# A hybrid attention and gMLP block: own buffer rings for the raw tiles and operands of a Strassen MLP, and an output projection with one PSUM bank for each half

## The chip, the cores and the metric

The kernel runs on one core of a Trainium2 chip. The metric is device time in microseconds (us) of one execution, as the median of several runs. One execution was also taken by the hardware profiler; its rows are what the text reads.

## What is computed

One layer over x of 2048 rows by 1024 columns, float32. Cut to what matters here:

```python
h = rmsnorm(x, norm_mix_g)
q, k, v, u, vg = split(h @ w_in)                      # five parts of 512 columns
a_out = stick_breaking_attention(q, k, v)             # 8 heads of 64, causal
b_out = spatial_gating(gelu(u), gelu(vg), ...)        # 8 groups of 64
mix = concat(rmsnorm(a_out, g[:512]), rmsnorm(b_out, g[512:]))
x = x + mix @ w_out                                   # 1024 x 1024
h = rmsnorm(x, norm_mlp_g)
x = x + square(relu(h @ w_up)) @ w_down               # 1024 -> 4096 -> 1024
return rmsnorm(x, norm_final_g)
```

## The kernel before

The rows are worked in four chunks of 512 (`TC`), each of four blocks of 128 (`NTB`). Matmul operands are split into a high and a low float32r part: `split` (lines 78 to 85) copies the high part on ScalarE (ACT, line 81) and subtracts for the low part on VectorE (line 82). `mm3` (lines 87 to 91) then makes three matmuls of 512 columns: high by high, high by low, low by high.

Work is written as Python generators, and `together(main, side, ratio)` steps a side generator `ratio` times for each `yield` of the main one. The program framework sorts each engine's instructions when the program is built, beginning from program order; an instruction whose inputs and buffer are ready may go ahead of an earlier one that still waits. All loads discussed here are issued on the queue of SyncE (SP), in the order that came out of this.

The order is: input projections of chunks 0 and 1; projections of chunks 2 and 3 with attention as the side; then, still beside attention, `Out(0)` and `Out(1)` (output projection and second norm), `up_plain` (first MLP layer of chunks 0 and 1), `Out(2)`, and `down_plain`; then `Out(3)` beside the rest of `down_plain`; and last the MLP of chunks 2 and 3 by a scheme of seven products (Strassen), `up_seven` and `down_seven`, with nothing beside it.

`Out` has three parts. `operands` loads `a_d` (transposed, 512 by 512) and `b_d`, squares `b` with a running sum (line 475), splits `a`, squares `a` (line 479), adds the squares of four tiles on GpSimd (POOL, lines 481 and 482), sums over partitions with a matmul against a column of ones (line 486), makes both inverse roots, multiplies `b`'s by the root of `a`'s mean (lines 490 to 493), scales `b` on ACT (line 498), transposes it on TensorE (line 501) and splits it. `product` loads the residual x (line 527), then for each half of 512 output columns loads both parts of `w_out` (line 512, or line 515 with a split for chunk 0, which also stores the split parts), and for each row block runs 24 matmuls of both parts into one PSUM bank, which VectorE adds to the residual with the scale of `a` (line 543). `turn` normalizes and transposes. A chunk may start only when attention has made the steps of that chunk (the `while steps[0]` loops).

A `Room` hands out buffers from rings by name; a ring serves its tiles in program order, and a tile waits until a slot is free:

```python
rm = Room(None, None, dict(w8=9, s12=1, t8=12, acts=2, t2=2), dict(w8=hx, s12=hx))
```

In the Strassen stages `w8` (nine slots of 8 KB per partition) serves raw tiles, by `raw8`, and operands, by `w8`, alike. `Rights` holds the seven right operands of the up stage, the first of them (`hc[0]`) in two `w8` tiles, the others in `t8`. `Lefts` loads one raw tile of `w_up` for each `q` of 16 (line 717) and makes seven operands in four `w8` pairs. The products of a `q` are 12 matmuls each; `keep_acts` sums and stores the result to `s_d` (lines 583 to 587). `down_seven` has four groups `g` of seven products (`ORDER_D`). Each product loads a raw tile from `s_d` (line 857) and splits it and a `w_down` combination into four `w8` tiles: two for the first half of its contraction, two for the second. It then runs 48 matmuls into four banks, and VectorE adds these to accumulators (lines 826 to 831). At the start of a group POOL makes three differences for each half (lines 847 to 849), later one more (line 851). The raw tiles of `w_down` come from `t8` (line 808), in odd groups half of them from `w8`. `y_d` is loaded at line 819. In the last group the last two products run row block by row block, and `finish` writes the output.

Of the kernel before, what the change touches and what calls it, by code (L numbers as in the profile page):

```python
# [8 lines left out]
F32 = mybir.dt.float32  # L9
F32R = mybir.dt.float32r  # L10
BF16 = mybir.dt.bfloat16
AF = mybir.ActivationFunctionType
ALU = mybir.AluOpType
# [3 lines left out]
P = 128  # L17
# [4 lines left out]
SBW = 512  # L22
DFF = 4096
TC = 512
NTB = TC // P
NC = T // TC
KD = D // P
EPS = 1e-6
# [6 lines left out]
def block_kernel(ctx: ExitStack, tc: tile.TileContext, x, x_t, gmix, w_in, ln_g, ln_b, sgw, sgb,  # L35
                 outg, w_out, gmlp, w_up, w_down, gfin, out):
    nc = tc.nc
# [14 lines left out]
    ones = const.tile([P, 1], F32, name="ones")  # L52
    nc.gpsimd.memset(ones, 1.0)
    mhalf = const.tile([P, NTB], F32, name="mhalf")
# [11 lines left out]
    b_d = dram.tile([T, SBW], F32, name="b_d")  # L66
    wi_d = dram.tile([5, KD // 2, P, 2, 2, 512], F32, name="wi_d")
    wo_d = dram.tile([2, 2, 2, P, 4, 512], F32, name="wo_d")

    def rsqrt_mean(pool, ssq, n, count, tag):  # L70

        m = pool.tile([P, NTB], F32, name=f"{tag}_m", bufs=2)
        nc.vector.tensor_scalar(m[:, :n], ssq, 1.0 / count, EPS, ALU.mult, ALU.add)  # L73
        r = pool.tile([P, NTB], F32, name=f"{tag}_r", bufs=2)
        nc.gpsimd.tensor_tensor(r[:, :n], m[:, :n], mhalf[:, :n], ALU.pow)  # L75
        return r
# [10 lines left out]
    def mm3(ps, lh, ll, rh, rl, first, last, more=False):  # L87

        nc.tensor.matmul(ps, lh, rh, start=first, stop=False, skip_group_check=more)  # L89
        nc.tensor.matmul(ps, lh, rl, start=False, stop=False, skip_group_check=more)  # L90
        nc.tensor.matmul(ps, ll, rh, start=False, stop=last, skip_group_check=more)  # L91
# [332 lines left out]
    class Room:  # L424
# [9 lines left out]
        def w8(self, shape):  # L434
            return self.get("w8", shape, F32R)

        def raw8(self, shape):
            return self.get("w8", shape)

        def t8(self, shape, dtype=F32):  # L440
            return self.get("t8", shape, dtype)
# [13 lines left out]
    def split4(hl, src):  # L455
        for j in range(0, 4, 2):
            split(hl[0][:, j:j + 2, :], hl[1][:, j:j + 2, :], src[:, j:j + 2, :])

    class Out:
# [3 lines left out]
            self.c, self.rm = c, room  # L463

        def operands(self):

            rm, c = self.rm, self.c
            at = rm.t8([4, TC])
            nc.sync.dma_start(at, a_d[:, c * TC:(c + 1) * TC].rearrange("(n p) t -> p n t", p=P))
            st = rm.t8([4, SBW])  # L470
            nc.sync.dma_start(st, b_d[c * TC:(c + 1) * TC, :].rearrange("(n p) d -> p n d", p=P))
            ssq = rm.small("rb_ssq", NTB)
            for tb in range(NTB):
                sq = rm.t4([SBW], BF16)
                nc.scalar.activation(sq, st[:, tb, :], AF.Square, accum_out=ssq[:, tb:tb + 1])
            am = self.am = rm.pair([4, TC])
            split4(am, at)
            yield
            nc.scalar.activation(at, at, AF.Square)
            total = rm.pool.tile([P, TC], F32, name="a_sq", bufs=1)  # L480
            nc.gpsimd.tensor_tensor(at[:, 0:2, :], at[:, 0:2, :], at[:, 2:4, :], ALU.add)
            nc.gpsimd.tensor_tensor(total, at[:, 0, :], at[:, 1, :], ALU.add)
            rb = rsqrt_mean(rm.pool, ssq, NTB, SBW, "rb")
            pssq = rm.ps()
            for tb in range(NTB):
                nc.tensor.matmul(pssq[:, tb:tb + 1], total[:, tb * P:(tb + 1) * P], ones, start=True, stop=True)
            m = rm.small("ra_m", NTB)
            nc.vector.tensor_scalar(m, pssq[:, :NTB], 1.0 / SBW, EPS, ALU.mult, ALU.add)
            ra = rm.small("ra", NTB)
            nc.gpsimd.tensor_tensor(ra, m, mhalf[:, :NTB], ALU.pow)  # L490
            root = rm.small("ra_root", NTB)
            nc.gpsimd.tensor_tensor(root, m, ra, ALU.mult)
            nc.gpsimd.tensor_tensor(rb, rb, root, ALU.mult)
            self.ras = [ra[:, tb:tb + 1] for tb in range(NTB)]
            yield
            bm = self.bm = rm.pair([4, TC])
            for tb in range(NTB):
                nc.scalar.activation(st[:, tb, :], st[:, tb, :], AF.Copy, scale=rb[:, tb:tb + 1])
                ps = rm.ps((P, 4, P))
                for e in range(4):  # L500
                    nc.tensor.transpose(ps[:, e, :], st[:, tb, e * P:(e + 1) * P], ident)
                ts_ = slice(tb * P, (tb + 1) * P)
                split(bm[0][:, :, ts_], bm[1][:, :, ts_], ps)
                yield

        def weights(self, half, part):

# [13 lines left out]
        def product(self):  # L521
            rm, c = self.rm, self.c
            self.ys = []
            for t2 in range(2):
                y = rm.t8([2, D])
                r0 = c * TC + t2 * 2 * P
                nc.sync.dma_start(y, x[r0:r0 + 2 * P, :].rearrange("(n p) d -> p n d", p=P))
                self.ys += [y[:, 0, :], y[:, 1, :]]
            ys = self.ys

            for half in range(2):
                ws = [self.weights(half, part) for part in range(2)]
                hs = slice(half * 512, (half + 1) * 512)
                for tb in range(NTB):
                    ts_ = slice(tb * P, (tb + 1) * P)
                    ps = rm.ps()
                    for part, m in ((0, self.am), (1, self.bm)):
                        for e in range(4):
                            mm3(ps, m[0][:, e, ts_], m[1][:, e, ts_], ws[part][0][:, e, :], ws[part][1][:, e, :],
                                part == 0 and e == 0, part == 1 and e == 3)  # L540
                            if e == 1 or part == 0 and e == 3:
                                yield
                    nc.vector.scalar_tensor_tensor(ys[tb][:, hs], ps, self.ras[tb], ys[tb][:, hs], ALU.mult, ALU.add)
                    if half == 1:
                        nc.sync.dma_start(y_d[c][:, tb, :], ys[tb])
                    yield
                if c == 0:
                    for part in range(2):
                        for i in range(2):
                            nc.sync.dma_start(wo_d[half, part, i], ws[part][i].bitcast(F32))  # L550

        def turn(self):

# [122 lines left out]
    class Rights:  # L676


        def __init__(self, rm):

            self.rm, self.hc = rm, [None] * 7
            self.b11, self.t2, self.b12, self.b21, self.b22 = (rm.raw8([4, TC]) for _ in range(5))
            b11 = self.b11
            for t, src in ((b11, h_d[0][0]), (self.b12, h_d[1][0]), (self.b22, h_d[1][1]), (self.b21, h_d[0][1])):
                nc.sync.dma_start(t, src)
            self.keep(0, b11, rm.w8)
            self.minus(b11, self.b12, b11)
            self.minus(self.t2, self.b22, b11)
            self.minus(self.b12, self.b22, self.b12)
# [21 lines left out]
    class Lefts:  # L711


        def __init__(self, rm, q):
            self.rm, self.pair, self.n = rm, None, 0
            st = rm.raw8([2, 2, 512])
            nc.sync.dma_start(st, w_up[2 * q:2 * q + 2].rearrange("f p (h k) c -> p f h (k c)", h=2))
            a11, self.a12, self.a21, self.a22 = st[:, 0, 0], st[:, 0, 1], st[:, 1, 0], st[:, 1, 1]
            self.a11, self.s = a11, rm.get("s12", [512])
            nc.gpsimd.tensor_tensor(self.s, self.a21, self.a22, ALU.add)  # L720
            self.w0, self.w4 = self.operand(a11), self.operand(self.s)

        def operand(self, src):
            if self.n % 2 == 0:
                self.pair = self.rm.w8([2, 2, 512])
            w = self.pair[:, self.n % 2]
            self.n += 1
            split(w[:, 0, :], w[:, 1, :], src)
            return w
# [64 lines left out]
    class Down:  # L794
# [5 lines left out]
        def load(self, g):  # L800

            self.bs = []
            for h in range(2):
                v = []
                f0 = (8 * g + 4 * h) * P
                for n in range(2):
                    st = self.rm.raw8([4, 512]) if g % 2 and h else self.rm.t8([4, 512])
                    nc.sync.dma_start(st, w_down[f0:f0 + 4 * P, n * 512:(n + 1) * 512].rearrange("(f p) d -> p f d", p=P))
                    st = st.rearrange("p (j e) d -> p j e d", e=2)
                    v += [st[:, :, 0], st[:, :, 1]]  # L810
                self.bs.append([v[0], v[2], v[1], v[3]])
# [190 lines left out]
        for part in (o.operands, o.product, o.turn):  # L1002
            together(part(), down, 0.8)
    hx = ctx.enter_context(tc.tile_pool(name="hx", bufs=1, side="right", reuse_waits="tile"))
    rm = Room(None, None, dict(w8=9, s12=1, t8=12, acts=2, t2=2), dict(w8=hx, s12=hx))
    rights = Rights(rm)
    ahead = Lefts(rm, 0)
    together(down)
# [46 lines left out]
```

## Time and profile before

| | us |
|---|---|
| median of 3 runs (lowest, highest) | 2624.02 (2620.88, 2625.3) |
| the profiled execution, device time | 2620.27 |
| the profiled execution, span of its instructions | 2618.6 |
| TensorE busy | 2454.1 |
| VectorE busy | 1684.6 |
| ScalarE busy | 1158.5 |
| mean granted TensorE clock | 0.972 of full speed |

The span runs from the first to the last instruction of the profiled execution. Busy time counts instructions at work on an engine. The granted clock is what the chip allowed TensorE, as a share of full speed; TensorE is either at its full 2.4 GHz or at 1.2 GHz, so 0.77 in a stretch means that it was at the lower level for 46% of it. PE is TensorE, PEld its weight loads, DVE VectorE, ACT ScalarE, POOL GpSimd, SPq the queue on which SyncE issues transfers.

### The profile page before, as it was taken

To read this page: it belongs to the slowest core of one execution; us is meant where nothing else is said; L and a number is where in the kernel's file an instruction comes from. 1 tells how busy PE (TensorE), PEld (TensorE's weight loads), DVE (VectorE), ACT (ScalarE), POOL (GpSimd) and SP (SyncE) were. 2 spreads that over 40 slices of the span, in tenths; PEclk is the share of its full clock that TensorE was granted. 3 is DMA by queue.
4 is the path that set the end of the run, shared out by engine and by line. 5 is a ranking of instruction groups with operands and counts; after the bars stand their busy time and mean duration, and the time that the engine had idled before them with its cause. 6 is when DMAs were issued, how large, how long until landed. Compare 5 with 4: busy or idle time off the path is not lost. (4 is left out here: it accounts for less than half of the span.)

```text
span 2618.6 us, 30138 instructions
## 1 busy us (share of the span) xinstructions
PE 2454.1 (94%) x11328; PEld 1985.7 (76%) x11328; DVE 1684.6 (64%) x2236; ACT 1158.5 (44%) x2020; POOL 315.4 (12%) x259
## 2 busy tenths in 40 slices
PE   8899898997979999999999899999989999799997
PEld 7787677775757888888877688788767888687875
DVE  3643557868675666666666688635566665468877
ACT  4422335536454555555564454313134544233333
POOL 1100000101010000000010000000023323213330
PEclk9999999998989999999999899999999999999998
DMA  9637788677654343333364633346223344753332
GB/s 374 244 125 219 215 255 261 205 221 224 244 190 157 121 121 121 121 124 122 121 236 162 197 121 113 122 156 241 96 81 142 140 161 149 261 206 116 113 113 113
DMA packets 158225, 446.58 MB, mean 171 GB/s; under 512 B 12544, under 2 KB 28928, under 8 KB 138624
## 3 DMA queue, kind: packets, MB, share of 16 engines
q1 hardware_dynamic: 149744, 417.39, 47.8%
q0 software_dynamic: 4032, 25.17, 2.4%
q10 hardware_dynamic: 4304, 2.10, 0.3%
q8 instruction: 90, 1.47, 0.2%
q14 instruction: 55, 0.45, 0.1%
HBM read 314.59 MB, written 130.02 MB: 170 GB/s over the span
## 5 line engine op out<-in xcount | busy, mean ns | idle before, releaser
L89 PE MATMUL mm<-t,t 128*128 128x512 f32 x1280 | 499.5, 394 | 4.5 <-DVE t L664 4.5
L91 PE MATMUL mm<-t,t 128*128 128x512 f32 x1280 | 502.3, 393 | 0.0
L90 PE MATMUL mm<-t,t 128*128 128x512 f32 x1280 | 501.9, 392 | 0.3 <-DVE t L82 0.3
L359 DVE TENSOR_TENSOR_SCAN pr<-kk,pr,zeros 128x513 f32<-128x513 f32 x192 | 248.3, 1293 | 117.3 <-ACT kk L351 116.9
L351 ACT ACTIVATE kk<-z 128x512 f32<-128x512 f32 (+2 forms) x320 | 171.5, 536 | 334.5 <-PE z L346 187.8
L89 PEld LDWEIGHTS mm<-t,t 128*128 128x128 f32 x1280 | 242.3, 190 | 55.6 <-DVE t L664 4.9
L90 PEld LDWEIGHTS mm<-t,t 128*128 128x128 f32 x1280 | 241.9, 189 | 51.4 <-DVE t L82 1.1
L91 PEld LDWEIGHTS mm<-t,t 128*128 128x128 f32 x1280 | 241.5, 189 | 51.6
L81 ACT ACTIVATE w<-w 128x512 fp32r<-128x512 f32 (+1 forms) x150 | 121.1, 825 | 299.6 <-DMA w<-s_d 172.3
L82 DVE TENSOR_TENSOR w<-w,w 128x512 fp32r<-128x512 f32 (+1 forms) x150 | 176.5, 1191 | 88.7 <-ACT w L81 86.8
L370 PE MATMUL tr<-ident,b 128*128 128x128 f32 x1088 | 186.3, 283 | 43.7 <-DVE aT L82 30.0
L90 PE MATMUL mm<-w,w 128*128 128x512 f32 x512 | 204.1, 399 | 17.3 <-DVE w L82 17.3
L82 DVE TENSOR_TENSOR aT<-tr,aT 128x512 fp32r<-128x512 f32 (+1 forms) x320 | 190.9, 599 | 35.7 <-ACT aT L81 35.6
L89 PE MATMUL mm<-w,w 128*128 128x512 f32 x512 | 201.4, 396 | 12.4 <-ACT w L81 11.5
L81 ACT ACTIVATE aT<-tr 128x512 fp32r<-128x512 f32 (+1 forms) x320 | 172.6, 541 | 90.2 <-PE tr L370 89.7
L91 PE MATMUL mm<-w,w 128*128 128x512 f32 x512 | 202.8, 396 | 0.0
L370 PEld LDWEIGHTS tr<-ident,b 128*128 128x128 f32 x1088 | 133.6, 144 | 90.7 <-DVE aT L82 38.8
L81 ACT ACTIVATE t<-t 128x1024 fp32r<-128x1024 f32 x104 | 105.7, 1060 | 179.1 <-DMA t<-in_w_down 112.8
L353 ACT ACTIVATE b<-z 128x512 f32<-128x512 f32 (+2 forms) x320 | 171.3, 535 | 0.5 <-PE tr L370 0.5
L356 DVE TENSOR_TENSOR_SCAN pr<-kk,zeros 128x128 f32<-128x128 f32 (+3 forms) x128 | 105.5, 826 | 90.8 <-ACT kk L351 90.3
L89 PE MATMUL mm<-t,w 128*128 128x512 f32 x384 | 154.0, 401 | 8.9 <-DVE acts L775 4.7
L388 PE MATMUL av<-aT,vt 128*128 128x512 f32 (+1 forms) x320 | 144.5, 452 | 13.7 <-DMA vt<-v_d 3.5
(192 smaller groups left out, 4629.3 us busy)
## 6 DMA issues: line engine op xcount, KB each, us to landing
w_in<-wi_d SPq DMA_DIRECT2D x40, 1024.0 KB, 8.0
kt<-k_d SPq DMA_DIRECT2D x160, 256.0 KB, 4.9
t<-in_w_down SPq DMA_DIRECT2D x28, 1024.0 KB, 6.6
s_d<-acts SPq DMA_DIRECT2D x16, 1792.0 KB, 6.2
w<-s_d SPq DMA_DIRECT2D x28, 1024.0 KB, 4.8
t<-wo_d SPq DMA_DIRECT2D x24, 1024.0 KB, 8.7
wi_d<-w_in POOLq DMA_DIRECT2D x20, 1024.0 KB, 8.0
vt<-v_d SPq DMA_DIRECT2D x80, 256.0 KB, 2.9
```

The lines of the kernel that those rows point to most:

```text
L81: nc.scalar.activation(hi, src, AF.Copy)
L82: nc.vector.tensor_tensor(lo, src, hi.bitcast(F32), ALU.subtract)
L89: nc.tensor.matmul(ps, lh, rh, start=first, stop=False, skip_group_check=more)
L90: nc.tensor.matmul(ps, lh, rl, start=False, stop=False, skip_group_check=more)
L91: nc.tensor.matmul(ps, ll, rh, start=False, stop=last, skip_group_check=more)
L351: nc.scalar.activation(kk[:, :L], z[:, :L], AF.Sigmoid, scale=-QK_SCALE)
L353: nc.scalar.activation(b[:, :L], z[:, :L], AF.Sigmoid, scale=QK_SCALE)
L356: nc.vector.tensor_tensor_scan(pr[:, L - 1::-1], kk[:, L - 1::-1], zeros[:, :L], 1.0, ALU.mult, ALU.add)
L359: nc.vector.tensor_tensor_scan(pr[:, ::-1], kk[:, ::-1], zeros, carry[tb], ALU.mult, ALU.add)
L370: nc.tensor.transpose(tr[:, tb * P:(tb + 1) * P], bs[tb][:, j * P:(j + 1) * P], ident)
L388: nc.tensor.matmul(av[:, t0:], vt[:, j, :], aT[:, 0, t0:], start=first, stop=False)
```

## The change

In the Strassen stages the nine slots are cut into three rings: five `w8` for operands, two `raw8` for raw tiles, two `x8` for `hc[0]` and, in odd groups of the down stage, for half of the `w_down` raw tiles. The first operand pair of the up stage stands in `raw8`.

In `Out`, the weights of the first product group are asked for first, then `b_d`, then `a_d`. `b` is transposed unscaled, its norm made block by block. The sum of squares of `a` is made by 16 matmuls that accumulate on TensorE. The product runs in four groups, each of one half of the columns and one part of the contraction (`b` first); each row block of a group has a bank of its own for 12 matmuls, and VectorE adds it to the residual with the norm of that part.

```diff
-        def raw8(self, shape):
-            return self.get("w8", shape)
+        def raw8(self, shape, dtype=F32):
+            return self.get("raw8", shape, dtype)
+
+        def x8(self, shape, dtype=F32R):
+            return self.get("x8", shape, dtype)
...
         def operands(self):
-
             rm, c = self.rm, self.c
+            self.rbs = []
+            self.ready = [self.weights(0, 1)]
+            st = rm.t8([4, SBW])
+            nc.sync.dma_start(st, b_d[c * TC:(c + 1) * TC, :].rearrange("(n p) d -> p n d", p=P))
             at = rm.t8([4, TC])
             nc.sync.dma_start(at, a_d[:, c * TC:(c + 1) * TC].rearrange("(n p) t -> p n t", p=P))
-            st = rm.t8([4, SBW])
-            nc.sync.dma_start(st, b_d[c * TC:(c + 1) * TC, :].rearrange("(n p) d -> p n d", p=P))
-            ssq = rm.small("rb_ssq", NTB)
+            bm = self.bm = rm.pair([4, TC])
             for tb in range(NTB):
                 sq = rm.t4([SBW], BF16)
-                nc.scalar.activation(sq, st[:, tb, :], AF.Square, accum_out=ssq[:, tb:tb + 1])
-            am = self.am = rm.pair([4, TC])
-            split4(am, at)
-            yield
-            nc.scalar.activation(at, at, AF.Square)
-            total = rm.pool.tile([P, TC], F32, name="a_sq", bufs=1)
-            nc.gpsimd.tensor_tensor(at[:, 0:2, :], at[:, 0:2, :], at[:, 2:4, :], ALU.add)
-            nc.gpsimd.tensor_tensor(total, at[:, 0, :], at[:, 1, :], ALU.add)
-            rb = rsqrt_mean(rm.pool, ssq, NTB, SBW, "rb")
...
-                nc.scalar.activation(st[:, tb, :], st[:, tb, :], AF.Copy, scale=rb[:, tb:tb + 1])
+                ssq = rm.small("rb_ssq")
+                nc.scalar.activation(sq, st[:, tb, :], AF.Square, accum_out=ssq)
+                m = rm.small("rb_m")
+                nc.vector.tensor_scalar(m, ssq, 1.0 / SBW, EPS, ALU.mult, ALU.add)
+                rb = rm.small("rb", bufs=2 * NTB)
+                nc.gpsimd.tensor_tensor(rb, m, mhalf[:, 0:1], ALU.pow)
+                self.rbs.append(rb)
                 ps = rm.ps((P, 4, P))
                 for e in range(4):
                     nc.tensor.transpose(ps[:, e, :], st[:, tb, e * P:(e + 1) * P], ident)
                 ts_ = slice(tb * P, (tb + 1) * P)
                 split(bm[0][:, :, ts_], bm[1][:, :, ts_], ps)
                 yield
+            am = self.am = rm.pair([4, TC])
+            split4(am, at)
+            nc.scalar.activation(at, at, AF.Square)
+            pssq = rm.ps()
+            for tb in range(NTB):
+                for e in range(4):
+                    nc.tensor.matmul(pssq[:, tb:tb + 1], at[:, e, tb * P:(tb + 1) * P], ones, start=e == 0, stop=e == 3)
+            ra = rsqrt_mean(rm.pool, pssq[:, :NTB], NTB, SBW, "ra")
+            self.ras = [ra[:, tb:tb + 1] for tb in range(NTB)]
+            yield
...
-            for half in range(2):
-                ws = [self.weights(half, part) for part in range(2)]
+            def group(half, part, m, rr):
+                ws = self.ready.pop() if self.ready else self.weights(half, part)
                 hs = slice(half * 512, (half + 1) * 512)
                 for tb in range(NTB):
                     ts_ = slice(tb * P, (tb + 1) * P)
                     ps = rm.ps()
-                    for part, m in ((0, self.am), (1, self.bm)):
-                        for e in range(4):
-                            mm3(ps, m[0][:, e, ts_], m[1][:, e, ts_], ws[part][0][:, e, :], ws[part][1][:, e, :],
-                                part == 0 and e == 0, part == 1 and e == 3)
-                            if e == 1 or part == 0 and e == 3:
-                                yield
-                    nc.vector.scalar_tensor_tensor(ys[tb][:, hs], ps, self.ras[tb], ys[tb][:, hs], ALU.mult, ALU.add)
-                    if half == 1:
+                    for e in range(4):
+                        mm3(ps, m[0][:, e, ts_], m[1][:, e, ts_], ws[0][:, e, :], ws[1][:, e, :], e == 0, e == 3)
+                        if e == 1:
+                            yield
+                    nc.vector.scalar_tensor_tensor(ys[tb][:, hs], ps, rr[tb], ys[tb][:, hs], ALU.mult, ALU.add)
+                    if half == 1 and part == 0:
                         nc.sync.dma_start(y_d[c][:, tb, :], ys[tb])
                     yield
...
+            yield from group(0, 1, self.bm, self.rbs)
+            yield from group(0, 0, self.am, self.ras)
+            yield from group(1, 1, self.bm, self.rbs)
+            yield from group(1, 0, self.am, self.ras)
...
-            self.b11, self.t2, self.b12, self.b21, self.b22 = (rm.raw8([4, TC]) for _ in range(5))
+            self.b11, self.t2, self.b12, self.b21, self.b22 = (rm.get("w8", [4, TC]) for _ in range(5))
...
-            self.keep(0, b11, rm.w8)
+            self.keep(0, b11, rm.x8)
...
-                self.pair = self.rm.w8([2, 2, 512])
+                self.pair = self.rm.raw8([2, 2, 512], F32R) if self.first and self.n == 0 else self.rm.w8([2, 2, 512])
...
-                    st = self.rm.raw8([4, 512]) if g % 2 and h else self.rm.t8([4, 512])
+                    st = self.rm.x8([4, 512], F32) if g % 2 and h else self.rm.t8([4, 512])
...
-    rm = Room(None, None, dict(w8=9, s12=1, t8=12, acts=2, t2=2), dict(w8=hx, s12=hx))
+    rm = Room(None, None, dict(w8=5, raw8=2, x8=2, s12=1, t8=12, acts=2, t2=2),
+              dict(w8=hx, raw8=hx, x8=hx, s12=hx))
```

## Rows read from the trace of the kernel before

**Rows 1.** The page, busy time of TensorE: us, share of the span, instructions.

```profile
PE 2454.1 (94%) x11328; PEld 1985.7 (76%) x11328; DVE 1684.6 (64%) x2236; ACT 1158.5 (44%) x2020; POOL 315.4 (12%) x259
```

**Rows 2.** Busy time by stretch: stretch, length, engines, PEclk, DMA share, GB/s.

```profile
613.00:660.00 47.00, 32.26 (x151) 23.92 (x151) 42.15 (x64) 34.97 (x72) 7.94 (x8) 0.79 0.83 262
725.00:770.00 45.00, 29.95 (x128) 20.76 (x127) 37.29 (x52) 29.09 (x58) 8.08 (x7) 0.77 0.77 252
840.00:1315.00 475.00, 474.94 (x2348) 391.43 (x2348) 307.88 (x390) 265.93 (x504) 8.78 (x8) 1.00 0.39 121
1345.00:1372.00 27.00, 20.58 (x106) 15.63 (x106) 20.45 (x29) 15.52 (x30) 1.94 (x3) 0.94 0.98 352
1975.00:2255.00 280.00, 279.98 (x1221) 228.91 (x1220) 173.68 (x231) 133.53 (x228) 82.11 (x56) 1.00 0.42 149
2255.00:2300.00 45.00, 29.09 (x103) 22.45 (x103) 24.19 (x23) 15.45 (x19) 16.47 (x7) 0.77 0.75 288
2360.00:2385.00 25.00, 22.62 (x98) 17.72 (x97) 22.46 (x17) 7.57 (x9) 18.95 (x6) 1.00 0.24 85
2520.00:2580.00 60.00, 50.16 (x208) 40.57 (x207) 51.30 (x48) 18.71 (x19) 21.55 (x8) 0.91 0.23 84
```

**Rows 3.** Timeline of chunk 1's `Out`: start, us, engine, line, operation, idle before.

```profile
730.64 0.38 SPq L469 DMA_DIRECT2D t<-a_d  x1
...
751.32 1.87 PE L486 MATMUL mm<-ones,a_sq 128*128 128x1 f32 x8 [1.99 <-POOL a_sq L482]
...
756.13 1.95 ACT L498 ACTIVATE t<-t,rb_r 128x512 f32<-128x512 f32 x3 [6.55 <-POOL rb_r L493]
...
771.74 0.86 PE L89 MATMUL mm<-t,t 128*128 128x512 f32 x3
```

**Rows 4.** Timeline of the SP queue in chunk 0's `Out`.

```profile
613.90 0.87 SPq L469 DMA_DIRECT2D t<-a_d  x1
...
640.40 0.46 SPq L515 DMA_DIRECT2D t<-in_w_out  x1
```

**Rows 5.** Timeline of the SP queue from the up stage into the down stage.

```profile
2236.96 0.34 SPq L857 DMA_DIRECT2D w<-s_d  x1
2249.06 0.37 SPq L808 DMA_DIRECT2D t<-in_w_down  x1
...
2272.19 0.37 SPq L587 DMA_DIRECT2D s_d<-acts  x1
2272.64 2.99 SPq L819 DMA_DIRECT2D t<-y_d  x3
2275.68 46.41 SPq L857 DMA_DIRECT2D w<-s_d  x5
```

**Rows 6.** Timeline of ACT, VectorE and TensorE at the start of the down stage.

```profile
2265.58 1.06 ACT L81 ACTIVATE w<-t 128x1024 fp32r<-128x1024 f32 x1 [0.53 <-DMA t<-in_w_down]
...
2272.04 1.21 DVE L82 TENSOR_TENSOR w<-t,w 128x1024 fp32r<-128x1024 f32 x1
...
2273.30 0.79 PE L90 MATMUL mm<-w,w 128*128 128x512 f32 x1 [4.37 <-DVE w L82]
...
2292.49 1.65 PE L89 MATMUL mm<-w,w 128*128 128x512 f32 x3 [11.54 <-ACT w L81]
```

**Rows 7.** Timeline of VectorE in the last group of the down stage.

```profile
2547.63 5.01 DVE L831 TENSOR_TENSOR t<-t,t 128x512 f32<-128x512 f32 x6
```

**Rows 8.** Timeline of VectorE and ACT at a product's end, and beside POOL.

```profile
2304.74 2.73 DVE L828 TENSOR_TENSOR t<-mm,t 128x512 f32<-128x512 f32 x4 [4.04 <-PE mm L91]
2306.11 1.06 ACT L81 ACTIVATE w<-w 128x1024 fp32r<-128x1024 f32 x1 [7.99 <-PE mm L91]
...
2446.18 3.41 DVE L82 TENSOR_TENSOR w<-w,w 128x1024 fp32r<-128x1024 f32 x1
```

**Rows 9.** Timeline of the sums in chunk 2; the evacuations of the product by line.

```profile
1344.59 1.05 PE L486 MATMUL mm<-ones,a_sq 128*128 128x1 f32 x8
...
L543 DVE SCALAR_TENSOR_TENSOR t<-mm,ra,t x32: 741/751/752, 668.8 to 1788.1; 128x512 f32<-128x512 f32 x32
```

More of the change, by code (lines that the diff above doesn't have):

```diff
@@ L482, in operands @@
-            nc.gpsimd.tensor_tensor(total, at[:, 0, :], at[:, 1, :], ALU.add)
-            rb = rsqrt_mean(rm.pool, ssq, NTB, SBW, "rb")
[L484 to L494, printed above, removed]
-            yield
-            bm = self.bm = rm.pair([4, TC])
-            for tb in range(NTB):
-                nc.scalar.activation(st[:, tb, :], st[:, tb, :], AF.Copy, scale=rb[:, tb:tb + 1])
+                ssq = rm.small("rb_ssq")
+                nc.scalar.activation(sq, st[:, tb, :], AF.Square, accum_out=ssq)
@@ L536, in product @@
                     ps = rm.ps()
-                    for part, m in ((0, self.am), (1, self.bm)):
-                        for e in range(4):
-                            mm3(ps, m[0][:, e, ts_], m[1][:, e, ts_], ws[part][0][:, e, :], ws[part][1][:, e, :],
-                                part == 0 and e == 0, part == 1 and e == 3)
-                            if e == 1 or part == 0 and e == 3:
-                                yield
-                    nc.vector.scalar_tensor_tensor(ys[tb][:, hs], ps, self.ras[tb], ys[tb][:, hs], ALU.mult, ALU.add)
-                    if half == 1:
+                    for e in range(4):
[4 more added lines that the diff above has]
+                    if half == 1 and part == 0:
                         nc.sync.dma_start(y_d[c][:, tb, :], ys[tb])
@@ L547, in product @@
                 if c == 0:
-                    for part in range(2):
-                        for i in range(2):
-                            nc.sync.dma_start(wo_d[half, part, i], ws[part][i].bitcast(F32))
+                    for i in range(2):
+                        nc.sync.dma_start(wo_d[half, part, i], ws[i].bitcast(F32))
+            yield from group(0, 1, self.bm, self.rbs)
+            yield from group(0, 0, self.am, self.ras)
+            yield from group(1, 1, self.bm, self.rbs)
+            yield from group(1, 0, self.am, self.ras)
         def turn(self):
@@ L714, in __init__ @@
         def __init__(self, rm, q):
-            self.rm, self.pair, self.n = rm, None, 0
+            self.rm, self.pair, self.n, self.first = rm, None, 0, q == 0
             st = rm.raw8([2, 2, 512])
```

## Prediction

> **What bounds the kernel now.** I read the page first: TensorE is busy 94% of the span [rows 1], so only what it loses counts, idle time and time at the lower of its two clock levels (1.2 GHz instead of 2.4). The table by stretch shows where that is [rows 2]. In 840:1315 us and in the Strassen up stage, 1975:2255, TensorE is busy without a break at clock 1.00; nothing but fewer matmuls helps there. It loses time where the change works. Idle is length minus busy time: 14.7 us in 613:660, 15.1 in 725:770 and 6.4 in 1345:1372, the stretches from the loads of `Out` to its first product matmuls in chunks 0, 1 and 2 (36.2 us together); then 15.9 in 2255:2300, 2.4 in 2360:2385 and 9.8 in 2520:2580, the down stage.
>
> Next I read one `Out` in order of time, chunk 1 [rows 3]. `a_d` is asked for at 730.6, the sums of squares reach TensorE at 751.3 after the POOL adds, the scaling of `b` that needs both norms starts at 756.1, the first product matmul at 771.7. For 41 us TensorE has almost nothing but attention steps. In chunk 0 the first weight load is issued at 640.4, 26.5 us after that of `a_d` [rows 4]. The reader is to see that dense matmuls are missing there, not that attention got slower.
>
> Last the down stage. The queue's rows show the first raw tile loaded at 2237, well ahead, but the second (product 1) issued only at 2275.7, behind a store of `acts` that could not go before 2272.2 and three loads of `y_d` [rows 5]. TensorE, done with product 0 just before 2281, stands for 11.5 us until its first operand is split [rows 6].
>
> **The change, part by part.** The profiled execution took 2620.3 us (span 2618.6), and I sum against that. The three runs shown have a median of 2624.0, 3.7 above it; I add this at the end.
>
> *Rings.* A raw tile of product n+1 has waited for one of nine shared slots, two of which `hc[0]` holds in the up stage. With two slots for raw tiles alone, product 0 takes the slot of `q`=14's tile and product 1 that of `q`=15's. The latter is free once its last operand is split, for which a pair slot opens when `q`=14 has about done its sixth product of seven. A `q` takes 19 us (84 matmuls of 0.229 us, 280 us by 1221 [rows 2]) and `q`=15 ends near 2263, so this is about 2243, and the load stands ahead of the late store. That a load may pass stores of earlier lines is seen in the same rows: product 0's stands well before that store, though its line comes later [rows 5]. Saved: 11.5 us, and something for the clock. 0.77 over 45 us means 20.7 at the lower level, of which the idle covers at most 15.9, so 5 us or more of matmuls ran at half speed; I take 2.5. Together 14.
>
> A later raw tile has, with two slots, a whole product of 48 matmuls (11.0 us) to be loaded in. I credit the 2.4 us of 2360:2385, and of the 9.8 in 2520:2580 the 2.5 that a late tile cost. Not the rest, 7.3 near 2555, when VectorE works off additions to `ys`, six of them 5.0 us [rows 7], which remain. Together 4.9.
>
> Against it: five slots for operands, four per product. The last operand of product n+1 can be split only when product n has ended, and is needed after 24 matmuls, 5.5 us. From the end on: ACT 1.06 us; VectorE's four additions out of PSUM last until 1.4 us after it (2304.74 and 2.73, against 2306.1); then the low half, 1.2 us; ready at 2.7. While POOL subtracts, a low half takes up to 3.4 us; ready at 4.8 [rows 8]. So the middle of a group costs nothing. At its start POOL runs six subtractions and several such halves queue up: I take 0.75 us for each of four groups, 3. The last product of the last group needs all four operands for its first row block and finds three of them unsplit; 3 for it (a high and two low halves, less what other row blocks fill), and 1 for the tail. The two `x8` loads of group 1 can leave once `hc[0]` is free, near 2246, ahead of group 0's. At 288 GB/s [rows 2] their 2 MB take 7.3 us, 4.6 more than the gap before the next loads, so the split of 2265.6 would come at 2270.2: still before 2272.0, when VectorE is through with `acts` and takes it up [rows 6]. No cost; without that cover 4.6.
>
> Down stage: -14 - 4.9 + 3 + 3 + 1 = -12 us. Bounds: -33 (28.1 us of idle and 5 of clock, all regained) and +18 (no credit but the 14, and 32 for twelve products that meet POOL each late by 2.7: one contended half more, 4.8 + 3.4 - 5.5).
>
> The Trainium skill, page "SBUF — State Buffer", section "Who interferes with whom", says that a VectorE instruction with two SBUF inputs and a GpSimd instruction that reads SBUF shut each other out for a whole instruction. By that a low half may wait out a subtraction of some 3.3 us and then run its 1.2: ready at 5.9 us, 0.4 late, about 5 us over the twelve products where my sum has 3. The row's 3.4 is less than such a wait and its run together, and I keep the row.
>
> The up stage holds its first raw tile and first pair in the two raw slots, where they had two of the nine. With TensorE full there it is priced 0.
>
> *Output projection.* Gone: the scaling of `b` (three calls 1.95 us), two POOL adds, and the wait of the transposes for both norms. The transposes now need only the load of `b`, and the first product group only `b` and weights that are asked for before `a_d`; the other norm has that whole group (48 matmuls, 11 us, and four attention steps) to arrive. So dense matmuls start some 25 us earlier in chunks 0 and 1.
>
> Added on TensorE: 16 sums instead of 4 for each chunk, two passes each, 24 passes more. Eight take 1.05 us, 0.11 apart [rows 9]: 2.7 a chunk, 10.6 in all. Added on VectorE: 8 more evacuations of 0.75 us for each chunk [rows 9], 24 us. It is busy 37.3 of 45 us in 725:770, but the group evacuated has other banks behind it and TensorE work to hide it; I charge 3. Without that cover, 24.
>
> Gain: two thirds of the 36.2 us idle, 24, since the attention that must end before a chunk starts still runs thin. The three stretches had 43.6 us at the lower level (0.42 by 47, 0.46 by 45, 0.12 by 27). With TensorE busy 70% of it (82.8 of 119) that cost 15; half is 7.5. Sum: -24 - 7.5 + 10.6 + 3 = -18. Bounds: -41 (36.2 and 15 regained, 10.6 paid) and +35 (nothing regained, 10.6 and 24 paid).
>
> Total -30: 2590 for such an execution, 2594 for the median.
>
> **Rivals.** (1) *Only the rings gain.* Attention between chunks is paced by VectorE, so idle taken from one stretch comes back in the next. For it: VectorE is busy 42 of 47 us in 613:660. Against: 840:1315 holds the same attention with TensorE full. `Out` comes to 0: 2624 - 12 = 2612. (2) *Only the projection gains*, because product 1's load lands behind the store as before and the new waits are paid: 2624 - 18 - 4.9 + 7 = 2607. Against: the slot count above. (3) *Nothing moves*: what `Out` regains goes to sums and evacuations, what the raw ring regains to operand waits: 2624. (4) *Slower: VectorE binds in `Out`.* Place: the product groups of the four chunks, with scans, splits and now twice the evacuations. If it sets the pace, nothing idle is regained, and 10.6 and 24 are paid: 2624 - 12 + 35 = 2647. It decides once more than a third of that 35 is paid with nothing regained, which the 12 of the rings no longer cover. For it: the 42 of 47. Against: with the same attention steps in 840:1315 it is busy only 308 of 475.
>
> **How the numbers follow.** Both gains: 0.56, with its own range 2572 to 2609. Rival 1: 0.17. Rival 2: 0.08. Rival 3: 0.06. Rival 4 or operands at their worse bound: 0.13. About 0.2% (5 us) is what a measurement of this kernel can tell from no change. Faster is the first three, 0.81, less 0.01 for an edge of rival 1: 0.80. Same: 0.07. Slower: 0.13. The range leaves out 2 in 10: all of rival 4, part of rival 3 and the best end; 2564 (60 of the 74 us that both best bounds make) to 2621.
>
> **What would show it.** Right: product 1's load issued before 2250 and no wait over 5 us behind product 0; in chunk 1 the first product matmul within some 25 us of `a_d`'s load; less than 15 us idle in the three stretches; 128 passes of the sums. Wrong: TensorE waiting for a low half in the middle of products; idle and clock between chunks as before (rival 1); product 1's load behind the store (rival 2); group 1's loads crowding group 0's so that product 0 stands longer than the 4.4 us [rows 6] it stands now.

## The result, and the profile after

The changed kernel takes 2587.94 us (median of 4 runs, 2582.19 to 2588.74), the kernel before, beside it, 2623.05: a ratio of 0.9861, interval 0.9844 to 0.9878, 36 us faster. The prediction was 2594, 2564 to 2621, faster. The sum came out; its two terms did not: the rings brought twice what was predicted, the projection two thirds.

The page of the changed kernel, busy line, answers [rows 1]:

```profile
PE 2461.0 (95%) x11424; PEld 2001.7 (77%) x11424; DVE 1709.0 (66%) x2280; ACT 1152.8 (45%) x2004; POOL 307.6 (12%) x255
```

The span is 2587.0 us, 31.6 less. TensorE is busy 6.9 us *more*, with 96 passes more, so idle time fell by 38.5. The table by stretch, columns as in [rows 2]; the last three stretches are moved to follow the work:

```profile
613.00:660.00 47.00, 36.67 (x176) 29.57 (x176) 34.93 (x58) 32.27 (x66) 5.30 (x6) 0.78 0.93 308
725.00:770.00 45.00, 38.29 (x170) 31.20 (x169) 28.52 (x46) 18.05 (x38) 5.43 (x5) 0.82 0.60 189
1345.00:1372.00 27.00, 23.65 (x93) 19.34 (x93) 16.46 (x21) 9.46 (x15) 1.39 (x1) 0.75 0.62 214
...
2245.00:2300.00 55.00, 48.59 (x200) 38.70 (x199) 44.74 (x36) 20.64 (x24) 25.17 (x8) 0.94 0.76 288
2350.00:2375.00 25.00, 24.09 (x107) 19.62 (x106) 20.92 (x23) 9.29 (x10) 12.55 (x4) 1.00 0.32 112
2500.00:2560.00 60.00, 56.97 (x248) 45.97 (x248) 52.84 (x59) 20.62 (x21) 19.51 (x6) 1.00 0.19 71
```

In the three stretches of `Out` 20.4 us are idle (10.3, 6.7, 3.4) where [rows 2] had 36.2. But the clock is not regained: at twice one minus the clock, 20.7, 16.2 and 13.5 us ran at 1.2 GHz, 50.4 together, where it was 43.6. In the down stage both are regained: idle is 10.4 us in the last three lines against 28.1, and the clock back to 0.94 and 1.00 from 0.77 and 0.91.

Chunk 1's `Out` in order of time (SP queue, TensorE, VectorE; line 475 loads `a_d`, 488 transposes `b`, 498 is the sums, 89 the product) answers [rows 3]:

```profile
730.01 0.38 SPq L475 DMA_DIRECT2D t<-a_d  x1
...
735.26 0.60 PE L488 MATMUL mm<-ident,t 128*128 128x128 f32 x4
...
745.27 6.82 PE L498 MATMUL mm<-ones,t 128*128 128x1 f32 x32
...
751.95 0.77 PE L89 MATMUL mm<-t,t 128*128 128x512 f32 x1
...
752.12 0.16 DVE L73 TENSOR_SCALAR ra_m<-mm 128x4 f32<-128x4 f32 x1 [6.72 <-PE mm L498]
```

The first product matmul comes 21.9 us after the load, not 41.1. But see what stands right ahead of it: the last transposes of `b` end before 736, its last low half is ready at 737.5, and the weights were asked for ahead of `a_d`; the first product group needs nothing else. It follows the sums of `a` all the same, because line 498 is written ahead of `product` and stands ahead of it in TensorE's order (the run with the sums later, below, shows this). The sums wait for `a`, take 6.82 us, and keep VectorE idle for 6.72.

The SP queue into the down stage answers [rows 5]; line 856 loads raw tiles:

```profile
2233.13 0.33 SPq L856 DMA_DIRECT2D raw<-s_d  x1
2236.97 0.37 SPq L807 DMA_DIRECT2D x<-in_w_down  x1
...
2263.76 0.37 SPq L586 DMA_DIRECT2D s_d<-acts  x1
2264.22 2.99 SPq L818 DMA_DIRECT2D t<-y_d  x3
2267.25 5.71 SPq L856 DMA_DIRECT2D raw<-s_d  x2
```

TensorE there, answering [rows 6], and all that it waits for from 2235 to the end (total us, times, longest):

```profile
2264.88 0.79 PE L90 MATMUL mm<-w,w 128*128 128x512 f32 x1 [3.46 <-DVE w L82]
2283.98 0.97 PE L89 MATMUL mm<-w,w 128*128 128x512 f32 x3 [1.24 <-ACT w L81]
...
PE mm L90 <- DVE w L82: 9.1, 7, 3.5
PE mm L89 <- ACT w L81: 2.3, 3, 1.2
PE mm L90 <- DVE nf_m L73: 1.6, 1, 1.6
```

Product 0's tile is asked for at 2213.9 and product 1's at 2233.1, ahead of the late store, and the 11.54 us wait behind product 0 is gone. The 1.24 us at 2283.98 stand behind product 1: it is now product 2's tile, asked for at 2267.25, that comes behind the store and the loads of `y_d`; its first split, on ACT at 2281.92, waits 8.7 us for it. The last store of `acts` comes 8.4 us earlier than in [rows 5] (2263.76 against 2272.19); the other 23.2 of the 31.6 us are gained behind it.

### The profile page after: what moved, and what is told of

The parts are those of the page before. It is cut to its first block, busy times and chain, and to the rows that moved or that the text cites. A ratio compares the mean times of both kernels' runs of the same rounds, so it can differ in the third digit from the quotient of the medians.

```text
span 2587.0 us, 30340 instructions
## 1 busy us (share of the span) xinstructions
PE 2461.0 (95%) x11424; PEld 2001.7 (77%) x11424; DVE 1709.0 (66%) x2280; ACT 1152.8 (45%) x2004; POOL 307.6 (12%) x255
## 4 chain that ended last, share of the span: by engine, by line
PE 77%; DVE 13%; DMA 3%; issue 2%; ACT 2%; POOL 2%; SPq 0%; POOLq 0%; DVEq 0%; ACTq 0%
PE mm L91 21%; PE mm L90 21%; PE mm L89 21%; PE tr L370 4%; PE av L388 2%; PE av L389 2%; PE z L346 2%; PE z L345 2%; DVE pr L359 2%; DVE w L82 2%; DVE pr L356 1%; DVE aT L82 1%; DVE t L82 1%; DMA w_in<-wi_d 1%; PE mm L498 1%
## 5 line engine op out<-in xcount | busy, mean ns | idle before, releaser
L370 PEld LDWEIGHTS tr<-ident,b 128*128 128x128 f32 x1088 | 133.3, 143 | 79.0 <-DVE aT L82 28.1
L90 PE MATMUL mm<-w,w 128*128 128x512 f32 x448 | 176.5, 394 | 10.7 <-DVE w L82 9.1
L91 PE MATMUL mm<-w,w 128*128 128x512 f32 x448 | 175.4, 392 | 0.0
L89 PE MATMUL mm<-w,w 128*128 128x512 f32 x448 | 172.6, 391 | 2.3 <-ACT w L81 2.3
L82 DVE TENSOR_TENSOR w<-raw,w 128x512 fp32r<-128x512 f32 (+1 forms) x135 | 152.4, 1130 | 3.3 <-ACT w L81 2.8
L81 ACT ACTIVATE w<-raw 128x512 fp32r<-128x512 f32 (+1 forms) x135 | 106.4, 800 | 105.3 <-PE mm L91 85.8
L91 PE MATMUL mm<-t,w 128*128 128x512 f32 x380 | 149.7, 394 | 3.5 <-DVE w L82 3.5
L89 PE MATMUL mm<-t,w 128*128 128x512 f32 x380 | 150.7, 397 | 0.1
```

Source lines behind the costliest of these rows:

```text
L81: nc.scalar.activation(hi, src, AF.Copy)
L82: nc.vector.tensor_tensor(lo, src, hi.bitcast(F32), ALU.subtract)
L370: nc.tensor.transpose(tr[:, tb * P:(tb + 1) * P], bs[tb][:, j * P:(j + 1) * P], ident)
```

## Experiments

Each time is a median, beside runs of the kernel before on the same chip (2621.6 to 2622.3).

**The two parts alone.** `e1_rings` is the kernel before with the six edits of the rings; `e2_out` is the changed kernel with those undone.

> The kernel before with the rings alone (five slots for operands, two for raw tiles, two for `hc[0]` and then group 1's loads); `Out` as it was. Theory A, read from the markers of the two traces (the end moved by -31.6 us, of which -10 had come by the end of `down_plain`): the rings are worth 20 to 23 us, 2601 to 2604, and the half-speed stretch behind product 0 goes with the 11.5 us wait. Theory B, the sizes of the prediction: 12 us, 2612. Rival: the raw ring only pays when the projection also shifts the stores of `acts`: under 8 us, above 2616.

> The change without the rings: nine shared slots as before, new `Out`. Theory A (markers of the two traces): the projection is worth 10 to 13 us, 2611 to 2614, and TensorE still stands over 10 us behind product 0 of the down stage. Theory B, the sizes of the prediction: 18 us, 2606. If the two parts were not additive, this and the run of the rings alone would not sum to the 36 us by which the medians of before and after differ.

Rings alone: 2595.23, ratio 0.99 (0.9887 to 0.9914), 26 us faster. Projection alone: 2609.24, 0.9954 (0.9942 to 0.9967), 12 us. They sum to some 38 us, within the intervals of the whole (32 to 41), so the parts hardly touch; the projection alone keeps both large waits of the down stage, 10.7 and 7.8 us. The rings gave more even than theory A: with `Out` as it was, this run's last store of `acts` is already 3.1 us early (2269.09 against [rows 5]); 0.7 of it stood already at chunk 3's load of `a_d`, ahead of all that the rings touch. Some 2.4 came with the start of the up stage, which was priced 0: in 1900:1975 9.9 us are idle for 12.4.

```profile
2238.95 0.33 SPq L860 DMA_DIRECT2D raw<-s_d  x1
...
2269.09 0.37 SPq L590 DMA_DIRECT2D s_d<-acts  x1
```

**One raw slot instead of two**, on the changed kernel:

```diff
-    self.pair = self.rm.raw8([2, 2, 512], F32R) if self.first and self.n == 0 else self.rm.w8([2, 2, 512])
+    self.pair = self.rm.w8([2, 2, 512])
-rm = Room(None, None, dict(w8=5, raw8=2, x8=2, ...
+rm = Room(None, None, dict(w8=6, raw8=1, x8=2, ...
```

> The changed kernel with one slot for raw tiles and six for operands (the first pair of the up stage back among the operands). Theory A: what the rings bring is the lead of a whole product, which takes two raw slots; with one, a tile is asked for only when the last half of the tile before it is split, lands 4.8 us later, and again lands behind VectorE's additions: 10 to 20 us slower than the change, 2598 to 2608. Theory B: what matters is only that a raw tile no longer queues for a slot behind operands and the late store of `acts`; with six operand slots the last half is split in the middle of the product before, so the load still lands in time: 2584 to 2593.

2618.76, 0.9992 (0.9983 to 1.0001): with one slot the whole gain is lost, more than theory A said; it is also 9.5 us slower than the new `Out` with nine shared slots (2609.24), so a ring for raw tiles pays only with the second slot. Its SP queue, TensorE, VectorE in the last group, and waits:

```profile
2267.35 0.37 SPq L586 DMA_DIRECT2D s_d<-acts  x1
2267.80 3.00 SPq L818 DMA_DIRECT2D t<-y_d  x3
2270.86 1.26 SPq L856 DMA_DIRECT2D raw<-s_d  x1
...
2286.71 1.65 PE L89 MATMUL mm<-w,w 128*128 128x512 f32 x3 [12.08 <-ACT w L81]
...
2542.82 1.28 DVE L827 TENSOR_TENSOR t<-mm,t 128x512 f32<-128x512 f32 x2
2544.01 3.69 DVE L830 TENSOR_TENSOR t<-t,t 128x512 f32<-128x512 f32 x6
2547.62 1.21 DVE L82 TENSOR_TENSOR w<-raw,w 128x1024 fp32r<-128x1024 f32 x1
...
PE mm L90 <- DVE w L82: 20.2, 8, 7.8
```

Both large waits of the kernel before are back in their places: product 1's load behind the store, and 7.8 us in the last group, where the low half of a late tile is queued behind VectorE's additions to `ys` (line 830). In the changed kernel the same additions run, but four halves are done ahead of them, and of the wait 1.86 us are left:

```profile
2510.77 1.21 DVE L82 TENSOR_TENSOR w<-acts,w 128x1024 fp32r<-128x1024 f32 x1
2511.90 1.21 DVE L82 TENSOR_TENSOR w<-raw,w 128x1024 fp32r<-128x1024 f32 x1
...
2516.85 4.36 DVE L830 TENSOR_TENSOR t<-t,t 128x512 f32<-128x512 f32 x6
```

**Four operand slots instead of five** (three for raw tiles):

```diff
-    self.b11, self.t2, self.b12, self.b21, self.b22 = (rm.get("w8", [4, TC]) for _ in range(5))
+    self.b22 = rm.raw8([4, TC])
+    self.b11, self.t2, self.b12, self.b21 = (rm.get("w8", [4, TC]) for _ in range(4))
-rm = Room(None, None, dict(w8=5, raw8=2, x8=2, ...
+rm = Room(None, None, dict(w8=4, raw8=3, x8=2, ...
```

> The changed kernel with four slots for operands and three for raw tiles (`b22` of `Rights` in the third). It prices what the prediction charged for scarce operand slots (3 + 3 + 1 us with five). Theory A, that pricing: with four, the last two operands of a product are split only after the one before it has ended, the second ready some 2.4 us after the 2.7 us of the prediction, 5.1 of the 5.5 there are; beside POOL (4.8 and 3.4 us and more) it is 3 to 5 us late in two or three products of each group: 25 to 45 us slower than the change, 2613 to 2633. Theory B, slots are not scarce and five cost nothing that can be seen: under 8 us, 2584 to 2596.

2596.54, 0.9905 (0.9891 to 0.992), 9 to 11 us slower than the change (2587.94, and 2585.11 in a later run): just outside theory B, far from theory A. TensorE waits 16.1 us for low halves instead of 9.1, in as many places:

```profile
PE mm L90 <- DVE w L82: 16.1, 7, 5.5
PE mm L89 <- ACT w L81: 2.7, 3, 1.2
```

The wait in the second product of groups 1 to 3 doubles (1.82 to 1.87 us for 0.91 to 0.93) and that of product 0 is 5.5 us; the other products of groups 1 and 2 wait for nothing, so VectorE beside POOL is not the limit that theory A made it.

**The part of `a` behind half of the first product group**, chunks 0 to 2; the same work in another order:

```diff
             am = self.am = rm.pair([4, TC])          # split of a, squares, sums, ra:
             split4(am, at)                           # now a method left(), no longer
             ...                                      # at the end of operands()
                 for tb in range(NTB):
+                    if mid and tb == 2:
+                        mid()
+                        yield
...
-            yield from group(0, 1, self.bm, self.rbs)
+            yield from group(0, 1, self.left if c < 3 else None)
```

> The changed kernel, but in chunks 0 to 2 the split of `a`, its squares and their sums are issued after two of the four blocks of the first product group instead of ahead of it; same work. Theory A, TensorE's order holds the product back: in chunk 1 the transposes of `b` are done at 735.9 but the first product matmul stands behind the sums until 751.9; with the sums behind it the first product matmul comes near 740, and of the 20.4 us idle in the three stretches and some 12 us lost at the lower clock two thirds go: 2565 to 2575. Theory B, VectorE paces these stretches (busy 14.5 of 15 us in 730:745), so the blocks only trade places: 2585 to 2591.

2566.36, 0.9793 (0.9777 to 0.9809): 20 us faster than the change, as theory A had it. In chunk 1 `a_d` is asked for at 726.06; the product now follows the transposes:

```profile
731.32 0.60 PE L488 MATMUL mm<-ident,t 128*128 128x128 f32 x4
731.78 0.50 PE L89 MATMUL mm<-t,t 128*128 128x512 f32 x1
...
743.56 4.21 PE L506 MATMUL mm<-ones,t 128*128 128x1 f32 x32
```

**POOL sums**, in the change's place and in the later place, and **`b` loaded first**, in the later place:

```diff
+            nc.gpsimd.tensor_tensor(at[:, 0:2, :], at[:, 0:2, :], at[:, 2:4, :], ALU.add)
+            nc.gpsimd.tensor_tensor(total, at[:, 0, :], at[:, 1, :], ALU.add)
             for tb in range(NTB):
-                for e in range(4):
-                    nc.tensor.matmul(pssq[:, tb:tb + 1], at[:, e, tb * P:(tb + 1) * P], ones, ...)
+                nc.tensor.matmul(pssq[:, tb:tb + 1], total[:, tb * P:(tb + 1) * P], ones, ...)
```

> The changed kernel, with the squares of `a` summed by two POOL adds and four matmuls, as before the change, in place of sixteen matmuls. Theory A, the sums are dear: 24 passes fewer in each chunk at 0.215 us in chunks 0 to 2 (they ran at the lower clock) and 0.11 in chunk 3 are 18 us, 2570 to 2576. Theory B, TensorE has nothing else to do there and the adds (2.36 and 1.3 to 2.1 us) only move the wait: 2585 to 2591.

> The squares of `a` summed by two POOL adds and four matmuls, and the whole part of `a` behind two blocks of the first product group (chunks 0 to 2), both against the change. Measured on their own: 55.5 us (the place) and 42 us (POOL) faster than before, where the change was 36. Theory A: with product blocks ahead of the sums the adds are hidden, and TensorE saves the 96 passes at 0.11 us, 10.6 us more than the place alone: 2552 to 2558. Theory B: the two edits cure the same wait, since the POOL variant gained by leaving TensorE's order free sooner; together no more than the place alone: 2563 to 2569.

> The variant with `a` behind two blocks of the first product group (2566), and `b` loaded ahead of the first weights instead of behind them. Theory A: in chunk 0 the weights ahead of it made `b` land at 633.2, where it landed at 627.6 in the kernel before; the product can start that much sooner, and the attention has work to fill it: 3 to 6 us faster than that variant, 2560 to 2563. Theory B: the weights are then what the first product block waits for, or the attention steps fill the time anyway: 2564 to 2569.

POOL sums in place: 2579.70, 0.9837 (0.9822 to 0.9853); between the theories, and hardly apart from the change. In the later place: 2571.89, 0.9811 (0.9793 to 0.9829), no better than that place alone, and slower than either theory said: the adds give TensorE back some passes and a wait (2.45 us for them in chunk 0). `b` first: 2569.33, 0.9803 (0.9788 to 0.9817): the order of these loads is worth nothing that can be seen.

**Squares in bf16**, one pass a sum, in the change's place, in the later place, and in the old `Out` with the rings; and the change once more:

```diff
-    ones = const.tile([P, 1], F32, name="ones")
+    ones = const.tile([P, 1], BF16, name="ones")
-            nc.scalar.activation(at, at, AF.Square)
+            sq = rm.t4([4, TC], BF16)
+            nc.scalar.activation(sq, at, AF.Square)
-                    nc.tensor.matmul(pssq[:, tb:tb + 1], at[:, e, tb * P:(tb + 1) * P], ones, ...)
+                    nc.tensor.matmul(pssq[:, tb:tb + 1], sq[:, e, tb * P:(tb + 1) * P], ones, ...)
```

> The changed kernel with the squares of `a` written as bf16, so that a sum takes one pass instead of two: 16 passes a chunk instead of 32, in the same place; the squares are rounded to bf16 ahead of their sum. Theory A, the passes themselves cost, at the pace at which they ran (0.215 us in chunks 0 to 2, 0.12 in chunk 3), since the first product matmul stands right behind them: 3 x 3.4 + 2 = 12 us faster than the change, 2573 to 2579. Theory B, by the price of the prediction, 0.11 us each: 7 us, 2579 to 2584. Theory C, the stretch is set by what comes ahead of the sums: 2585 to 2590.

> The variant with `a` behind two blocks of the first product group (2566), with bf16 squares and one pass a sum. Theory A, the passes cost there too: 16 fewer in each chunk, at 0.11 to 0.16 us (32 of them took 3.4 to 4.9 us in that variant): 7 to 10 us faster than that variant, 2556 to 2560. Theory B, with product blocks on either side TensorE only trades them for waits elsewhere, as the POOL sums did there (2572): 2564 to 2572.

> The changed kernel once more, on the chip of these runs, as the measure for the small differences: 2583 to 2590.

> The kernel before with the rings (2595) and, in the old `Out`, the squares of `a` written as bf16 and summed by 16 one-pass matmuls instead of two POOL adds and four matmuls; one bank for both halves, `b` still scaled, weights last. It asks what the bank per half and the order of the loads are worth once sums are cheap; with them and the same sums the time was 2551. Theory A, the order carries the gain: the POOL adds took 3.7 to 4.5 us in a wait that stays (the scaling, the weights last), so 10 us or less: 2585 to 2595, and the order is worth the other 34 or more. Theory B, the sums were the wait: 20 us or more, under 2575.

The change again: 2585.11, 0.9866 (0.9853 to 0.988). With bf16 squares: 2550.92, 0.9733 (0.9718 to 0.9747), 34 us faster than that, three times theory A. Both: 2543.78, 0.9704 (0.9691 to 0.9717), the fastest of all kernels here, 78 us under the kernel before, and 23 us under the place alone, where theory A said 7 to 10; the place is worth 7 us once the sums are cheap. In the old `Out`: 2584.78, 0.9864 (0.9847 to 0.9882), 10 us under the rings alone: theory A, so with cheap sums the new order and the banks are worth 34 us (2584.78 to 2550.92).

The edit does a second thing. In the changed kernel ACT squares `a` in place, and so only when VectorE has subtracted the last low part from it, in chunk 1:

```profile
739.76 2.35 DVE L82 TENSOR_TENSOR t<-t,t 128x1024 fp32r<-128x1024 f32 x2
...
742.14 1.91 ACT L494 ACTIVATE t<-t 128x2048 f32<-128x2048 f32 x1 [0.88 <-DVE t L82]
```

The bf16 squares have a tile of their own and go beside or ahead of the subtraction (730.13 beside 729.34 to 731.67 in chunk 1; 1313.64 ahead of 1326.39 in chunk 2). From the load of `a_d` to the sums it is 19.8, 15.3, 25.0 and 20.3 us in the four chunks of the changed kernel and 18.3, 10.4, 15.8 and 18.6 here. No run has fp32 squares in a tile of their own, so how much of the 34 us is passes and how much the earlier start is not shown.

What the sums are, by their line, in the changed kernel (forms: count, ns least/median/most, first and last start; then who waited) and in the bf16 variant:

```profile
L498 PEld LDWEIGHTS mm<-ones,t x128: 187/333/337, 645.1 to 1707.9; 128*128 128x128 f32 x128
...
  DVE ra_m L73: 24.1, 4
```

```profile
L499 PEld LDWEIGHTS <-t x64: 95/96/114, 639.6 to 1670.9; 128*128 128x128 bf16 x64
...
  DVE ra_m L73: 1.3, 2
...
732.08 0.58 PE L499 MATMUL mm<-ones,t 128*128 128x1 bf16 x16 [1.83 <-ACT t L495]
```

## Why the prediction was right in sum and wrong in its terms

**The rings, -12 predicted, -26 measured.** The wait behind product 0 went as told (11.54 us to none; product 2 waits 1.24 us behind product 1), and product 1's load stood ahead of the store. Five operand slots cost about what was charged. In groups 1 to 3 one low half is late, by 0.91 to 0.93 us, half-way through the second product, and one by 0.85 at the start of group 0's third, 3.6 us together (3 charged). The last product waits 1.6 and 0.2 us for low halves (3 charged, and 1 for the tail; the view names the small VectorE instruction right behind the first of these halves).

Why a low half beside POOL takes 3.4 us, the prediction left open. In group 1 POOL's subtraction at 2340.20 takes 2.40 us, and the low half that VectorE starts beside it at 2340.94 ends at 2343.68, 1.1 us after it; then the two engines take turns, and an instruction of either lasts 3.25 to 3.42 us. The Trainium skill, page "SBUF — State Buffer", section "Who interferes with whom", calls the pair of ports that the two engines share an exclusive lock. The trace agrees with it. But the 5.9 us that the prediction worked out by that page counted one wait twice: a subtraction of 3.3 us holds POOL's own wait for VectorE, and the row's 3.4 is already a wait and a run together.

What failed in the rings' sum is the step "Not the rest, 7.3 near 2555, when VectorE works off additions to `ys` ... which remain". The additions remain and of the wait 1.86 us do: what was late was the raw tile, and one slot brings the wait back (7.8). Two smaller sizes were off. The down stage's clock was put at 2.5 us: in the lines of [rows 2] 31.5 us ran at 1.2 GHz (0.46 by 45, 0.18 by 60), after 6.6 (0.12 by 55), 24.9 less; 16.3 us of idle went with them (25.7 to 9.4), which leaves 8.6 us or more of matmuls that run at full speed again, 4.3 us gained at least. And the start of the up stage, priced 0, gives some 2.4. With 5.5 more for the late tile, 1.8 for the clock and 2.4, the -12 becomes -22; the rest of the 26 (interval 23 to 30) I can't place.

**The projection, -18 predicted, -12 measured.** Order and banks did better than was told, the sums worse. With cheap sums on both sides order and banks are worth 34 us, where -24 for idle, -7.5 for clock and +3 for evacuations, -28.5 together, had been put. The sums as they are, put at +10.6, cost 24: 34 in the new `Out` (2585.11 to 2550.92), less the 10 that cheap sums also gain in the old one (2595.23 to 2584.78). That these two errors nearly cancel is luck, and so is it that the rings' 14 us too few and the projection's 6 too many leave 36 beside the 30 of the sum.

The step that failed is "the other norm has that whole group (48 matmuls, 11 us, and four attention steps) to arrive": in the program the sums of `a` come ahead of the product, so TensorE held the product for `a` and then for the sums. The sign that I gave for it, the first product matmul within 25 us of the load, came true (21.9) and hid this. Behind half a group the same work is 20 us faster.

The mis-sized term is the sums: +10.6, from eight passes at 0.11 us [rows 9], a row at the full clock. [rows 3] has the same eight at 1.87 us in chunk 1, where the granted clock was 0.50. Here 32 passes took 6.8 us in chunks 0 to 2, 0.21 each, and 4.28 in chunk 3: 24.8 us, where those of before took 5.2, so 19.6 were added and not 10.6. With bf16 squares they are 0.54 to 0.58 a chunk, 2.2; that takes 22.5 us from TensorE, and 24.1 us of VectorE's waiting behind the sums becomes 1.3. The two profiled executions are 42.6 us of span apart (34 by the medians): TensorE's busy time on the page fell from 2461.0 to 2427.0 us, 34.0, of which the passes are 22.5, and idle time fell by 8.6; the other matmuls, as many as before, ran more at the full clock.

```profile
PE 2427.0 (95%) x11360; PEld 1970.5 (77%) x11360; DVE 1708.6 (67%) x2280; ACT 1151.6 (45%) x2004; POOL 308.5 (12%) x255
```

And with cheap sums the three stretches, moved to follow the work, look as the prediction meant them: 15.2 us idle, and 22.9 at 1.2 GHz instead of 50.4 (chunk 2's sums now stand just ahead of its stretch, at 1323.1).

```profile
613.00:660.00 47.00, 37.05 (x184) 29.21 (x183) 38.49 (x61) 29.75 (x58) 4.46 (x6) 0.89 0.98 326
713.00:758.00 45.00, 39.73 (x194) 31.59 (x194) 31.60 (x50) 19.80 (x41) 5.65 (x5) 0.86 0.59 210
1324.00:1351.00 27.00, 27.00 (x135) 22.46 (x134) 23.61 (x34) 11.75 (x23) 1.92 (x1) 1.00 0.91 318
```

What of this the cheap passes did, and what the earlier squares, is open as said above. The charge for the evacuations was not tried by itself.

**The other signs.** Product 0 stands 3.46 us, less than 4.4, so group 1's early loads did not crowd it. The 128 passes are there. Idle under 15 us was wrong (20.4), and the time at the lower clock between chunks stayed (50.4 us, 43.6 before), in part a sign of rival 1; these two pointed at the sums. A low half late in the middle of a product, a sign of wrong, came too, but at 0.9 us in each of three groups.

## What to carry to other kernels

A wait belongs to what was late, not to what the engine was doing then: VectorE's additions looked like the cause of a wait that a raw tile, one buffer slot short, had made. Work that only a later step needs must also be *written* later on an engine that keeps program order; a dependence removed on paper frees little while another waiting instruction stands ahead (writing the work later gave 20 us here). And price small matmuls at the clock of the stretch that they will run in, and by their weight loads: here one fp32 pass of a single column took TensorE 0.21 us at the lower clock, half of the 0.43 that a product matmul of 512 columns takes there.

## What the runs showed of the hardware

In the changed kernel an fp32 weight load of 128 by 128 for a one-column matmul took 187 ns at least and 333 in the median (in chunks 0 to 2 the sums ran at a granted clock of 0.50); in the bf16 variant it took 95 and 96. The passes followed each other 0.21 us apart (6.8 us for 32) in fp32 and 0.04 or less (0.58 for 16) in bf16. The Trainium skill, page "TensorE: Matmul & The Clock Gate", section "Weight-path perf modes — Fast Weight Load (FWL) and DoubleRow", says that the fast load is on for 128 weights of a type other than FP32; the rows agree.

Narrow passes were in some runs followed by a lower clock with TensorE busy throughout. In chunk 3 of the changed kernel the sums run from 1704.0 to 1708.3; the clock is 1.00, 0.99, then 0.50 (1.2 GHz). With bf16 squares, at the same place of the work, it stays at 1.00:

```profile
1690.00:1700.00 10.00, 10.00 (x54) 8.52 (x53) 5.47 (x12) 6.73 (x15) 2.16 (x4) 1.00 0.85 296
1700.00:1707.00 7.00, 7.00 (x46) 6.25 (x44) 4.74 (x5) 5.70 (x5) 0.00 (x0) 0.99 0.62 258
1707.00:1712.00 5.00, 5.00 (x16) 4.23 (x16) 0.76 (x2) 0.01 (x1) 1.01 (x1) 0.50 0.50 158
```

```profile
1670.00:1677.00 7.00, 7.00 (x46) 5.66 (x46) 4.29 (x7) 1.88 (x2) 1.94 (x1) 1.00 0.82 314
1677.00:1710.00 33.00, 33.00 (x147) 27.33 (x146) 11.78 (x16) 4.02 (x4) 0.00 (x0) 1.00 0.41 158
```

It is not so each time: of seven runs with these 32 fp32 passes in chunk 3 the clock fell in five, and in two, `e2_out` and the run with the part of `a` later, it was 1.00 during the passes (3.63 us) and behind them. What makes the difference stays open. In chunks 0 to 2 idle time came ahead of the sums as well, so what share of the lower clock there is the sums' stays open too.

VectorE and POOL took turns where both worked on SBUF: a subtraction of 128 by 1024 by VectorE takes 1.2 us alone and up to 3.42 beside POOL, one by POOL 2.40 at least and up to 3.40.
